# Rotating 96 images by 90 degrees: six hand-synchronised groups of 16 with 32 KB runs, in place of pooled tiles with 8 KB and 16 KB runs

## The chip, the cores and the metric

The kernel runs on one core of a Trainium2 chip. The metric is the device time of one execution in microseconds; a lower number is better. Before the change the median of three executions is 124.25 us.

## The reference

```python
x: float32 [32, 3, 256, 256]
out = np.rot90(x, k=1, axes=(-2, -1))     # out[.., i, j] = x[.., j, 255 - i]
```

96 images of 256 x 256 float32 (256 KB each) are rotated a quarter turn. No arithmetic is done: 25.17 MB are read and 25.17 MB are written, and every image is transposed and reversed along one axis on the way.

## The kernel before, in words

**Groups.** The 96 images are six groups of 16 images (4 MB each), and a group goes through three steps: DMAs bring it from DRAM into a tile `S` [128 partitions x 8192 float32], VectorE transposes `S` into a tile `U` of the same size, DMAs write `U` to DRAM. VectorE's transpose exchanges 32 partitions with 32 elements of the free dimension, so the access patterns `src` and `dst` choose which 32 elements meet and apply the reversal. `S` and `U` come from pools of three buffers each, so three groups can be in flight on either side. SyncE (SP) issues the loads, ScalarE (ACT) the stores; each has a DMA queue of its own, and both queues feed the same 16 DMA engines. In the profile the loads are queue q1 and the stores queue q10.

**Two kinds of group.** `KINDS = [1, 2, 2, 2, 2, 1]`.
- Kind 1 (the first and the last group): a partition holds 8 image rows, one run of 8 KB in DRAM. The group is cut into four quarters `s` of 1 MB: four loads (L50), four transposes of 128 x 2048 (L55), each followed by its store (L56). A quarter is transposed and stored as soon as it has landed.
- Kind 2 (the four groups between): a partition holds 16 image rows, one run of 16 KB. Two loads of 2 MB (L66), sixteen transposes of 128 x 512 (L71), each reading from both halves, then two stores of 2 MB (L73). The first transpose needs both loads.

**Zeros.** Ahead of the groups VectorE clears a tile `zero` [128 x 128] (L35) and ACT writes it, 64 KB in pieces of 512 B, to the part of the output that the last store overwrites at the end (L37).

**Order.** Tiles and semaphores are the tile framework's. It makes a load wait until the buffer that it overwrites was read, a transpose until its loads have landed and the old `U` was stored, and a store until its transposes are done. L88 and L99 are the framework's start and end.

Of the kernel before, what the change touches and what calls it, by code (L numbers as in the profile page):

```python
# [1 line left out]

# [4 lines left out]


@with_exitstack
def kernel(  # L10
    ctx: ExitStack,
    tc: tile.TileContext,
    x: bass.AP,
    out: bass.AP,
):
    nc = tc.nc
    B, C, H, W = x.shape
    assert H == W == 256
    N = B * C
    P = 128  # L20
    G = 16
    KINDS = [1, 2, 2, 2, 2, 1]
    assert len(KINDS) * G == N
    F = G * H * W // P
    fp32 = mybir.dt.float32

    xf = x.rearrange("b c h w -> (b c h w)").rearrange("(g f) -> g f", g=N // G)
    of = out.rearrange("b c h w -> (b c h w)").rearrange("(g f) -> g f", g=N // G)

    in_pool = ctx.enter_context(tc.tile_pool(name="in_pool", bufs=3))  # L30
    out_pool = ctx.enter_context(tc.tile_pool(name="out_pool", bufs=3))


    zero = ctx.enter_context(tc.tile_pool(name="zero", bufs=1)).tile([P, 128], fp32, name="zero")
    nc.vector.memset(zero[:], 0.0)  # L35
    last = of[N // G - 1].rearrange("(s p f) -> s p f", s=4, p=P)[3]
    nc.scalar.dma_start(out=last[:, :128], in_=zero[:])  # L37

    for g, kind in enumerate(KINDS):
        S = in_pool.tile([P, F], fp32, name="S")  # L40
        U = out_pool.tile([P, F], fp32, name="U")
        if kind == 1:

            R = 8
            Sv = S.rearrange("p (s f) -> p s f", s=4)
            Uv = U.rearrange("p (s f) -> p s f", s=4)
            xv = xf[g].rearrange("(s p f) -> s p f", s=4, p=P)
            ov = of[g].rearrange("(s p f) -> s p f", s=4, p=P)
            for s in range(4):
                nc.sync.dma_start(out=Sv[:, s], in_=xv[s])  # L50
            for s in range(4):

                src = Sv[:, s].rearrange("p (r k q) -> p q r k", r=R, q=R)[:, ::-1, :, ::-1]
                dst = Uv[:, s].rearrange("p (q k r) -> p q r k", q=R, r=R)
                nc.vector.transpose(dst, src)  # L55
                nc.scalar.dma_start(out=ov[s], in_=Uv[:, s])  # L56
        else:


            R = 16  # L60
            Sv = S.rearrange("p (b f) -> p b f", b=2)
            Uv = U.rearrange("p (a f) -> p a f", a=2)
            xv = xf[g].rearrange("(b a qk f) -> b qk a f", b=2, a=2, f=F // 2)
            ov = of[g].rearrange("(b a qk f) -> a qk b f", b=2, a=2, f=F // 2)
            for b in range(2):
                nc.sync.dma_start(out=Sv[:, b], in_=xv[b])  # L66

            src = Sv.rearrange("p b (r k q) -> p q r k b", r=R, q=R)[:, ::-1, :, ::-1]
            dst = Uv.rearrange("p a (q k r) -> p q r k a", q=R, r=R)
            for q in range(R):  # L70
                nc.vector.transpose(dst[:, q], src[:, q])  # L71
            for a in range(2):
                nc.scalar.dma_start(out=ov[a], in_=Uv[:, a])  # L73


# [1 line left out]
_INS = ['x']  # L77
_OUTS = [((32, 3, 256, 256), 'float32')]


# [23 lines left out]
```

## Time and profile before

| | |
|---|---|
| times of three runs | 124.26, 124.12, 124.25 us (median 124.25) |
| the profiled execution | 124.26 us, of which the span from first to last instruction is 122.5 us |
| VectorE busy | 91.5 us (75% of the span), 73 instructions |
| loads, queue q1 | 2304 packets, 25.17 MB |
| stores, queue q10 | 2448 packets, 25.23 MB (the zeros are in it) |
| moved over the span | 50.41 MB, mean 412 GB/s |

How to read it: the span is what the trace covers, and 1.76 us of the execution's time lie around it. The share of a DMA queue is the time that its packets took, added up over the 16 engines, as a share of 16 times the span. A packet here is one contiguous run of data, or a 4-byte semaphore write: each DMA adds 16 of those, one for each engine. The line of tenths cuts the span into 40 slices of 3.06 us. "To landing" is the time from the issue of a DMA to the semaphore that reports it complete. "Issue" is time in which an engine waited for nothing that the profile shows.

### The profile page before, as it was taken

What the parts mean: (1) busy time and instruction counts of PE and PEld (TensorE: products, weight loads), DVE (VectorE), ACT (ScalarE), POOL (GpSimd) and SP (SyncE); (2) the same over time, 40 slices, a digit from 0 to 9 for tenths busy, and PEclk for the clock granted to TensorE, in tenths of its full rate; (3) what the DMA queues carried; (4) which work ended last, traced back from release to release, by engine and by line L of the source; (5) the groups of instructions that cost most, each with busy time, mean ns of one, the idle gap of its engine ahead of it and who ended that gap; (6) DMA issues with size and microseconds to landing.
All of it is one profiled execution on the core that took longest, in us unless ns stands there. A gap on an engine that the chain in (4) does not pass through costs nothing.

```text
span 122.5 us, 173 instructions
## 1 busy us (share of the span) xinstructions
DVE 91.5 (75%) x73; POOL 0.2 (0%) x4
## 2 busy tenths in 40 slices
DVE  0199999006999999999999991699999999191000
POOL 0000000000000000000000000000000000000000
DMA  3999999999999999999999999999999999999994
GB/s 99 420 428 407 409 399 431 449 420 417 452 399 433 460 433 342 428 428 428 428 428 450 439 439 423 425 447 399 433 439 415 452 433 407 455 433 393 428 428 185
DMA packets 4753, 50.41 MB, mean 412 GB/s; under 512 B 528, under 2 KB 656, under 8 KB 656
## 3 DMA queue, kind: packets, MB, share of 16 engines
q1 hardware_dynamic: 2304, 25.17, 49.3%
q10 hardware_dynamic: 2448, 25.23, 48.4%
q14 instruction: 1, 0.01, 0.0%
HBM read 25.17 MB, written 25.23 MB: 411 GB/s over the span
## 4 chain that ended last, share of the span: by engine, by line
DMA 69%; DVE 20%; SPq 0%; issue 0%
DMA S<-in_x_dram 38%; DMA out_dram<-U 31%; DVE U L55 13%; DVE U L71 8%; SPq L50 0%
## 5 line engine op out<-in xcount | busy, mean ns | idle before, releaser
L71 DVE STREAM_TRANSPOSE U<-S 128x512 f32<-128x512 f32 x64 | 60.5, 1049 | 11.1 <-DMA S<-in_x_dram 7.4
L55 DVE STREAM_TRANSPOSE U<-S 128x2048 f32<-128x2048 f32 x8 | 31.0, 3948 | 7.2 <-DMA S<-in_x_dram 7.2
L35 DVE MEMSET zero<- 128x128 f32 x1 | 0.2, 165 | 0.8 <-PEq L88 0.8
L88 POOL MEMSET const-bfloat16-1.0<- 128x1 bf16 x1 | 0.1, 103 | 0.0
L88 POOL MEMSET const-uint8-127<- 128x1 uint8 x1 | 0.1, 103 | 0.0
L88 POOL MEMSET const-float32-1.0<- 128x1 f32 x1 | 0.1, 100 | 0.0
L88 POOL MEMSET const-float32-0.0<- 128x1 f32 x1 | 0.1, 99 | 0.2 <-issue 0.2
## 6 DMA issues: line engine op xcount, KB each, us to landing
S<-in_x_dram SPq DMA_DIRECT2D x8, 2048.0 KB, 21.5
out_dram<-U ACTq DMA_DIRECT2D x8, 2048.0 KB, 19.1
S<-in_x_dram SPq DMA_DIRECT2D x8, 1024.0 KB, 16.4
out_dram<-U ACTq DMA_DIRECT2D x8, 1024.0 KB, 15.9
out_dram<-zero ACTq DMA_DIRECT2D x1, 64.0 KB, 5.0
```

Of the source, the lines that this page charges most:

```text
L35: nc.vector.memset(zero[:], 0.0)
L55: nc.vector.transpose(dst, src)
L71: nc.vector.transpose(dst[:, q], src[:, q])
L88: nc = _bacc.Bacc("TRN2", target_bir_lowering=False, num_devices=1)
```

## The change

The pools and the framework's tracking go. Three buffers `S0..S2`, three buffers `U0..U2` and seven semaphores are named by hand: `loaded[s]` and `stored[u]` count DMA completions (16 each), `turned` counts groups that VectorE has finished. A block for hand-written code (`tile_critical`) stands around it all.

All six groups have one form now. Of each MB block `b` a partition of `S` holds 8 image rows, and the four blocks lie side by side in it: four loads of 1 MB. In the first group they are plain loads of 128 runs of 8 KB. In the other five the DRAM side of the load is written as 32 runs of 32 KB and the SBUF side as 128 partitions of 8 KB; since the usual call takes equal shapes on both sides, the instruction is built directly (`load`). VectorE turns a group in eight transposes of 128 x 1024, one for each image row `r` in a partition, each reading from all four blocks. A partition of `U` then holds 32 image rows, and one store of 4 MB writes 128 runs of 32 KB.

The waits: a load of group `g` from 3 on waits until group `g - 3` is turned; the first transpose of a group waits for its four loads and, from group 3 on, for the store of group `g - 3`; the store waits for the last of the eight transposes. At the end SP waits for all stores. The zeros (tile, clearing and write) are gone.

```diff
@@ -18,59 +18,77 @@
     assert H == W == 256
     N = B * C
     P = 128
-    G = 16
-    KINDS = [1, 2, 2, 2, 2, 1]
-    assert len(KINDS) * G == N
-    F = G * H * W // P
+    M = 4
+    G = 4 * M
+    RI, RO = 8, 8 * M
+    KO = H // RO
+    FI, FO = RI * W, RO * W
+    FOLD = 32
+    NG = N // G
+    NS = NU = 12 // M
     fp32 = mybir.dt.float32
 
-    xf = x.rearrange("b c h w -> (b c h w)").rearrange("(g f) -> g f", g=N // G)
-    of = out.rearrange("b c h w -> (b c h w)").rearrange("(g f) -> g f", g=N // G)
+    xf = x.rearrange("b c h w -> (b c h w)")
+    of = out.rearrange("b c h w -> (b c h w)")
 
-    in_pool = ctx.enter_context(tc.tile_pool(name="in_pool", bufs=3))
-    out_pool = ctx.enter_context(tc.tile_pool(name="out_pool", bufs=3))
+    xv = xf.rearrange("(g b d f) -> g b d f", g=NG, b=M, d=FOLD)
+    xp = xf.rearrange("(g b p f) -> g b p f", g=NG, b=M, p=P)
+
+    ov = of.rearrange("(g b qk f) -> g qk b f", g=NG, b=M, f=FO)
+
+    def fixed(ap):
+        return mybir.PhysicalAccessPattern(
+            ap=ap.ap, offset=ap.offset, dtype=ap.dtype, memref=ap.tensor.name,
+            memsetref=ap.tensor.name + "_set", bass_ap=ap,
+        )
+
+    def load(dst, src):
 
 
-    zero = ctx.enter_context(tc.tile_pool(name="zero", bufs=1)).tile([P, 128], fp32, name="zero")
-    nc.vector.memset(zero[:], 0.0)
-    last = of[N // G - 1].rearrange("(s p f) -> s p f", s=4, p=P)[3]
-    nc.scalar.dma_start(out=last[:, :128], in_=zero[:])
+        return nc.sync.add_instruction(
+            mybir.InstDMACopy(
+                name=nc.get_next_instruction_name(),
+                engine=mybir.EngineType.SP,
+                ins=[fixed(src)],
+                outs=[fixed(dst)],
+                queue="qSPDynamicHW",
+                mode="Copy",
+            )
+        )
 
-    for g, kind in enumerate(KINDS):
-        S = in_pool.tile([P, F], fp32, name="S")
-        U = out_pool.tile([P, F], fp32, name="U")
-        if kind == 1:
+    ctx.enter_context(tc.tile_critical())
+    S = [ctx.enter_context(nc.sbuf_tensor(f"S{i}", [P, M, FI], fp32)) for i in range(NS)]
+    U = [ctx.enter_context(nc.sbuf_tensor(f"U{i}", [P, FO], fp32)) for i in range(NU)]
+    loaded = [ctx.enter_context(nc.semaphore(f"loaded{i}")) for i in range(NS)]
+    stored = [ctx.enter_context(nc.semaphore(f"stored{i}")) for i in range(NU)]
+    turned = ctx.enter_context(nc.semaphore("turned"))
 
-            R = 8
-            Sv = S.rearrange("p (s f) -> p s f", s=4)
-            Uv = U.rearrange("p (s f) -> p s f", s=4)
-            xv = xf[g].rearrange("(s p f) -> s p f", s=4, p=P)
-            ov = of[g].rearrange("(s p f) -> s p f", s=4, p=P)
-            for s in range(4):
-                nc.sync.dma_start(out=Sv[:, s], in_=xv[s])
-            for s in range(4):
+    for g in range(NG):
+        s, u = g % NS, g % NU
+        if g >= NS:
+            nc.sync.wait_ge(turned, g - NS + 1)
+        for b in range(M):
+            if g == 0:
+                d = nc.sync.dma_start(out=S[s][:, b], in_=xp[g, b])
+            else:
+                d = load(S[s][:, b], xv[g, b])
+            d.then_inc(loaded[s], 16)
 
-                src = Sv[:, s].rearrange("p (r k q) -> p q r k", r=R, q=R)[:, ::-1, :, ::-1]
-                dst = Uv[:, s].rearrange("p (q k r) -> p q r k", q=R, r=R)
-                nc.vector.transpose(dst, src)
-                nc.scalar.dma_start(out=ov[s], in_=Uv[:, s])
-        else:
+        nc.vector.wait_ge(loaded[s], 16 * M * (g // NS + 1))
+        if g >= NU:
+            nc.vector.wait_ge(stored[u], 16 * (g // NU))
 
+        src = S[s][:].rearrange("p b (r k q) -> p r q k b", r=RI, q=RO)[:, :, ::-1, ::-1]
+        dst = U[u][:].rearrange("p (q k r) -> p r q k", q=RO, r=RI)
+        for r in range(RI):
+            t = nc.vector.transpose(dst[:, r], src[:, r])
+        t.then_inc(turned, 1)
 
-            R = 16
-            Sv = S.rearrange("p (b f) -> p b f", b=2)
-            Uv = U.rearrange("p (a f) -> p a f", a=2)
-            xv = xf[g].rearrange("(b a qk f) -> b qk a f", b=2, a=2, f=F // 2)
-            ov = of[g].rearrange("(b a qk f) -> a qk b f", b=2, a=2, f=F // 2)
-            for b in range(2):
-                nc.sync.dma_start(out=Sv[:, b], in_=xv[b])
+        nc.scalar.wait_ge(turned, g + 1)
+        nc.scalar.dma_start(out=ov[g], in_=U[u][:]).then_inc(stored[u], 16)
 
-            src = Sv.rearrange("p b (r k q) -> p q r k b", r=R, q=R)[:, ::-1, :, ::-1]
-            dst = Uv.rearrange("p a (q k r) -> p q r k a", q=R, r=R)
-            for q in range(R):
-                nc.vector.transpose(dst[:, q], src[:, q])
-            for a in range(2):
-                nc.scalar.dma_start(out=ov[a], in_=Uv[:, a])
+    for u in range(NU):
+        nc.sync.wait_ge(stored[u], 16 * len(range(u, NG, NU)))
 
 
 # ---- launch: one core; inputs and outputs as the reference has them ----
```

## The prediction

> **What bounds the kernel now.** The page comes first: is any resource full from end to end?
>
> ```profile
> span 122.5 us, 173 instructions
> DVE 91.5 (75%) x73; POOL 0.2 (0%) x4
> DVE  0199999006999999999999991699999999191000
> DMA  3999999999999999999999999999999999999994
> q1 hardware_dynamic: 2304, 25.17, 49.3%
> q10 hardware_dynamic: 2448, 25.23, 48.4%
> ```
>
> VectorE has holes; the DMA row has none between the first slice and the last. The queue shares add to 97.7% of 16 engines: 0.977 x 122.5 = 119.7 us of packets on each engine. The rest is start and end. The windows view of half microseconds places it:
>
> ```profile
> 1.00:1.50 0.50, 0.00 (x0) 0.00 (x0) 1.00 0.00 0
> 1.50:2.00 0.50, 0.00 (x0) 0.00 (x0) 1.00 0.49 131
> ...
> 120.50:121.00 0.50, 0.00 (x0) 0.00 (x0) 1.00 0.50 213
> 121.00:121.50 0.50, 0.00 (x0) 0.00 (x0) 1.00 0.09 33
> ```
>
> The last two columns are the DMA share and GB/s. Packets run from about 1.7 to about 121.3; 1.7 us lie before, 1.2 after. So the DMA engines set the time, and VectorE's 91.5 us hide beneath them. The chain of waits says so too: it is 69% DMA, and its VectorE pieces lie where the engines work on for other buffers.
>
> Next, what a packet costs and how the two queues share an engine. I asked for the DMA queues between 90 and 104 us, where loads are 8 KB packets (kind 1) and stores 16 KB (kind 2):
>
> ```profile
> q10 hardware_dynamic: 273, 3.95, 65.9%
> q1 hardware_dynamic: 275, 1.99, 33.6%
> ```
>
> Columns: packets, MB, share. Equal packets (32 of each are semaphore writes), twice the bytes: **the engines alternate packet by packet**, and a queue with smaller packets gets less. Shares times 16 x 14 us, over 243 and 241 data packets: 0.310 us for 8 KB, 0.612 us for 16 KB. The difference is 0.302 us per 8 KB, which leaves some 0.007 us fixed for each packet; 32 KB would take 4 x 0.302 + 0.007 = 1.216 us.
>
> Then VectorE, from the groups:
>
> ```profile
> L71 DVE STREAM_TRANSPOSE U<-S 128x512 f32<-128x512 f32 x64 | 60.5, 1049 | 11.1 <-DMA S<-in_x_dram 7.4
> L55 DVE STREAM_TRANSPOSE U<-S 128x2048 f32<-128x2048 f32 x8 | 31.0, 3948 | 7.2 <-DMA S<-in_x_dram 7.2
> ```
>
> 60.5/4 = 15.1 us for a kind 2 group and 31.0/2 = 15.5 us for a kind 1 group. Different strides, nearly the same price for an element, 1.85 to 1.89 ns.
>
> [...] the L71 transposes lie between 1021 and 1083 ns under full DMA traffic.
>
> **The change, part by part.**
>
> *DMA work.* Per engine, before: 64 + 64 packets of 8 KB at 0.309 and 64 + 64 of 16 KB at 0.611 make 117.8; 33 semaphore writes, 0.3; the zeros, 8 of 512 B, at most 0.2. Sum 118.3; the 119.7 of the page holds 1.4 us more, load packets that run slower than their floor. After: 32 of 8 KB (first group) are 9.9, 40 + 48 of 32 KB are 107.0, 30 semaphore writes 0.3: 117.2. So **1.1 us of packet time go**. The lower bound is 0.3 (if a widened load pays for four 8 KB writes, 40 x 0.024 = 1.0 comes back, and only the stores and zeros gain).
>
> *Memset, zeros' issue, pool waits.* The clearing is 0.165 us at L35, under the first load; its end is awaited only by the zeros' write. I take nothing beyond the packet time above.
>
> *The order of work.* Group 0 no longer starts transposing after 1 MB but after 4. By hand, with 15.3 us a group on VectorE:
> - Load 0 from 1.7 to 11.6, landed at 11.9. VectorE turns groups 0, 1, 2 back to back until 27.2, 42.5, 57.8.
> - Meanwhile loads 1 and 2 keep the engines full (8 x 1.216 = 9.7 us a group): load 1 lands at 21.6. Store 0 starts moving at 28.5 (1.3 us after its issue; the first load of before needed 0.73 to about 1.7), and halves load 2's rate: 33.8. So VectorE's later first start costs nothing, because three buffers of loads (29 us) cover it.
> - Now both queues always have work with 32 KB packets and alternate: 19.5 us for 4 MB on each. Loads 3, 4, 5 land at 53.2, 72.7, 92.1; stores 0, 1, 2 at 47.1, 66.6, 86.0. The load's new wait on `turned` holds SP only, with nothing else queued there, and comes due at 27.2, 42.5, 57.8, ahead of need.
> - VectorE: group 3 from 57.8 to 73.1, group 4 to 88.4, group 5 waits for its load and runs 92.2 to 107.5.
> - From 92.1 the engines have only stores. Left are 6.7 us of store 3 and 9.7 of store 4: to about 108.8. Store 5 is issued at 107.5 and moves at 108.8. **It comes just in time.** It ends at 118.6, the span at 119.8.
>
> The same arithmetic for before gives 1.7 + 118.3 + 1.2 = 121.2 against a true 122.5. I carry most of that remainder, 1.2, since loads run alone for longer here.
>
> *Entry and end of the hand-written block.* The program gains a branch and a no-op with a semaphore on SP, ACT and VectorE at both ends. Nothing in the trace prices it; what is there is the start, where the first DMA follows its branch within 0.1 us, and the end, 0.7 us of framework after the last landing. Between 0 and 1 us; I take 0.3. Less than nothing is excluded, as nothing of the framework's start and end is removed.
>
> Sum: 119.8 + 1.2 + 0.3 = 121.3 us of span, with 1.76 around it 123.1; a tenth for a gap ahead of store 5 gives **123.2 us**. The profiled execution (124.26) stands at the median (124.25), so no correction. A measurement here can tell about 0.2%, 0.25 us: under 124.0 is faster, over 124.5 slower.
>
> **The rivals.**
>
> *Loads still count as 8 KB packets* (slower). If the engine splits the widened read by its 8 KB writes, it sends 8 KB of load for 32 KB of store. For it: the SBUF side is 8 KB, and the 33.6% against 65.9% show what unequal packets do. [...] The stores run dry early and the loads are late: load 5 lands near 102.7 in place of 92.1. Group 5 has no pieces, so all that follows is bare: 15.3 of VectorE, 1.3 to first data, 9.7 of store, 1.2 of end: 130.3, with a remainder of 0.5 and 1.76, about **132.5 us**. It decides as soon as load 5 is later than about 92, since then the engines idle ahead of store 5.
>
> *VectorE's turn takes longer* (slower). The slack ahead of store 5 is about nil, but faster or slower turns also shift when loads are handed over; worked again with longer turns, no gap opens up to 15.9 us a group; from there each further microsecond of a group costs about 6, since all six follow one another. At 16.5 (2.0 ns an element) that is 123.2 + 3.4 = **126.6**. For it: the stride of 8 KB between the four blocks is new. Against it: kinds 1 and 2 differ in stride and hardly in price. An uneven sharing between the queues, or slower widened loads, would land in the same place, 125 to 129.
>
> *The change gives nothing* (same). Four writes are paid for each widened packet (+1.0) and entry and end cost 0.3 more than taken: **124.5 us**, between 123.8 and 124.8.
>
> **How the numbers follow.** Forecast 0.64, holding 122.2 to 124.6 (faster 0.54, same 0.06, slower 0.04). 8 KB packets 0.15, at 131 to 134, slower. VectorE or sharing 0.14, slower. Nothing gained 0.07 (0.02, 0.03, 0.02). So faster 0.56, same 0.09, slower 0.35. The range runs from 122.2 (no entry cost, half of the remainder) to 129, and leaves out the 8 KB case and the edges. The likeliest case alone: 122.2 to 124.6.
>
> **What would show it.** Right: q1's rate between 35 and 85 us equals q10's; DMA tenths of 9 throughout, also ahead of the last store; transposes near 1.9 us each, six groups of 15.3; group 5 starting near 92. Queue shares that add to less than before. Wrong: q1 at a fifth of the bytes in the shared stretch and a hole of ten microseconds near 110 (8 KB packets); eight transposes over 15.9 us and no wait for loads (VectorE); packets full but their total near 119.7 (nothing gained); a first DMA well after 1.0 us (entry).

## The result, and the profile after

The changed kernel takes 132.07 us (median of four runs, 131.71 to 136.57) against 124.19 before. The ratio is 1.0625, with a 95% interval of 1.0591 to 1.0658: slower by 7.8 us by the ratio, with the median 3.1 us above the upper end of the range forecast (129). A few runs here lie some 4 to 5 us above the others of the same kernel; ratios leave them out, medians don't, and the traces of `e4_tail_pieces` and `e10_store_2mb` are of such runs.

The page of the changed kernel, the lines that answer to those of before:

```profile
span 130.2 us, 134 instructions
DVE 91.0 (70%) x48; POOL 0.2 (0%) x4
...
DVE  0000999999999999999999607999900699990000
...
DMA  3999999999899999999999999999999997007973
...
q1 hardware_dynamic: 1536, 25.17, 46.1%
q10 hardware_dynamic: 864, 25.17, 44.9%
```

The DMA row has a hole that before had not, in the slices from about 107 to 120 us. The shares add to 91.0% of 130.2 us, 118.5 us on each engine, where before had 119.7 by the same sum. So the packets did become cheaper, by about what was forecast, and the engines stood idle for longer than that saved. The windows view places the idle stretch (columns: VectorE busy, POOL busy, clock, DMA share, GB/s):

```profile
108.00:110.00 2.00, 2.00 (x3) 0.00 (x0) 1.00 0.99 426
110.00:112.00 2.00, 2.00 (x2) 0.00 (x0) 1.00 0.08 33
112.00:114.00 2.00, 2.00 (x2) 0.00 (x0) 1.00 0.00 0
114.00:116.00 2.00, 2.00 (x2) 0.00 (x0) 1.00 0.00 0
116.00:118.00 2.00, 1.43 (x1) 0.00 (x0) 1.00 0.00 0
118.00:120.00 2.00, 0.00 (x0) 0.00 (x0) 1.00 1.16 492
```

While the engines stand still, VectorE turns the last group. The timeline says when it could begin (columns: start, length, engine, line, the idle time ahead and what ended it):

```profile
13.22 60.47 DVE L84 STREAM_TRANSPOSE U<-S 128x1024 f32<-128x1024 f32 x32 [13.22 <-DMA S<-in_x_dram]
...
78.82 15.24 DVE L84 STREAM_TRANSPOSE U<-S 128x1024 f32<-128x1024 f32 x8 [5.13 <-DMA S<-in_x_dram]
102.17 15.25 DVE L84 STREAM_TRANSPOSE U<-S 128x1024 f32<-128x1024 f32 x8 [8.11 <-DMA S<-in_x_dram]
```

Group 5 begins at 102.2 where the forecast had 92.2, and it waits for its load. From there everything is bare: 15.2 us of VectorE, 1.3 to the first packet, some 10 of store, 1.6 of end. **The loads came ten microseconds late.** Why is in the queues between 35 and 85 us, where both have work (packets, MB, share):

```profile
q10 hardware_dynamic: 422, 12.26, 56.8%
q1 hardware_dynamic: 432, 9.44, 43.9%
```

The number of packets is nearly the same again, but not the bytes. With 32 KB each, 9.44 MB are 288 data packets and 12.26 MB are 374. What fills up the 432 and the 422 are semaphore packets: 144 for the loads and 48 for the stores. The trace's packet records don't name the engine, but they show the order on one when each packet is put behind the one that ends where it starts, to within 4 ns (L, S: 32 KB of load or store; l, s: their 4-byte semaphore writes; one engine from 38 us on; the chains of the others run alike):

```
LSLSlSLSLSlsLSLSlSLSLSlSLSLSlsLSLSlSLSLSlSLSLSlsLS
```

A turn is the one packet that an engine takes from a queue before it goes to the other. After each two load packets (with a store packet between them and one behind) comes `l`, and after `l` a store packet: the 9 ns semaphore write takes the loads' turn and the store then has 1.2 us. A load of 1 MB is two data packets and one semaphore packet on an engine; a store of 4 MB is eight and one. So of three turns the loads use two for data, of nine the stores eight: 0.667 against 0.889, 42.9% of the bytes. Measured are 9.44/21.70 = 43.5%.

### The profile page after: what moved, and what is told of

Same layout as the page of the kernel before. It is cut to its first block, busy times and chain, and to the rows that moved or that the text cites. A ratio compares the mean times of both kernels' runs of the same rounds, so it can differ in the third digit from the quotient of the medians.

```text
span 130.2 us, 134 instructions
## 1 busy us (share of the span) xinstructions
DVE 91.0 (70%) x48; POOL 0.2 (0%) x4
## 4 chain that ended last, share of the span: by engine, by line
DVE 45%; DMA 40%; SPq 3%; issue 2%
DVE U L84 45%; DMA S<-in_x_dram 40%; SPq L48 2%; SPq L72 1%; SPq L117 0%; SPq L59 0%
## 5 line engine op out<-in xcount | busy, mean ns | idle before, releaser
L84 DVE STREAM_TRANSPOSE U<-S 128x1024 f32<-128x1024 f32 x48 | 91.0, 2060 | 26.5 <-DMA S<-in_x_dram 26.5
```

Source lines behind the costliest of these rows:

```text
L84: t = nc.vector.transpose(dst[:, r], src[:, r])
```

## The experiments

The theory to test: **the alternation gives a semaphore packet a whole turn, so the queue with more semaphores per byte loses.** It is called the turn theory below. Rivals: the widened load (32 runs of 32 KB read into 128 partitions) holds its own queue back, the widening theory; the loss is the last group's single piece, whatever the sharing, the tail theory.

### Stores of 1 MB (`e1_store_1mb`)

```diff
-        nc.scalar.dma_start(out=ov[g], in_=U[u][:]).then_inc(stored[u], 16)
+        for b in range(M):
+            nc.scalar.dma_start(out=ov[g][:, b], in_=U[u][b::M]).then_inc(stored[u], 16)
```

The waits on `stored` count four times as far.

> Each 4 MB store is cut into four of 1 MB (every fourth partition), so a store has 2 data packets and 1 semaphore packet per engine, as a load has. Turn theory (an engine's alternation gives a semaphore packet a whole turn, so the queue with more semaphores per byte loses): both queues move equal bytes in the shared stretch, load 5 lands near 94, the engines idle about 1 us, span 121.4, time 123.3. Widening theory (a read of 32 KB with four writes holds its queue back by itself): the loads keep about 43% of the bytes, time stays near 132. Tail theory (handing over the last group in one piece costs by itself, whatever the sharing): a hole near 110 stays, time near 132.

Measured: 124.35 us, ratio 1.0015 (0.9998 to 1.0031). Eighteen more DMAs, and 7.6 us less by the ratios. The queues from 35 to 80 us:

```profile
q1 hardware_dynamic: 446, 9.90, 51.3%
q10 hardware_dynamic: 433, 9.47, 48.9%
```

the DMA row of its page:

```profile
DMA  2999989899998989898999898999999999999991
```

and the last group in the timeline:

```profile
92.29 15.26 DVE L84 STREAM_TRANSPOSE U<-S 128x1024 f32<-128x1024 f32 x8 [3.44 <-DMA out_dram<-U]
```

The bytes are even, group 5 begins at 92.3, and it no longer waits for its load but for an old `U` to be stored. The DMA row has no hole. The loads are the same widened ones as in the changed kernel: the widening theory falls. VectorE turns the last group in the same one piece, and its stores wait for the end of it: the tail theory falls as a cause by itself. The span missed its mark, 122.3 for 121.4, and the time likewise; that is taken up below.

### One load of 4 MB for a group (`e11_one_load`)

```diff
-        for b in range(M):
...
-                d = load(S[s][:, b], xv[g, b])
-            d.then_inc(loaded[s], 16)
+            xg = xf.rearrange("(g p b f) -> g p b f", g=NG, b=M, p=P)[g]
+            nc.sync.dma_start(out=S[s][:], in_=xg).then_inc(loaded[s], 16)
```

Group 0 keeps its four loads.

> The other side of the 1 MB stores: the stores stay whole (8 data packets and 1 semaphore packet per engine) and the loads of groups 1 to 5 become one DMA of 4 MB each, 128 runs of 32 KB to 128 partitions, also 8 and 1. The rows then lie otherwise in the partitions, so the output isn't the rotation: that part of the computation is changed, the amount of data and the instructions of VectorE are not. Turn theory: equal bytes on both queues in the shared stretch, no hole, packet time about 118 per engine, time 124.2 like the 1 MB stores. A theory in which short stores let the loads in, and not the count of semaphores per byte, expects the sharing to stay at 43% and the time at 132.

Measured: 124.36 us, ratio 1.0014 (1.0005 to 1.0022). From 35 to 80 us:

```profile
q1 hardware_dynamic: 334, 9.90, 51.0%
q10 hardware_dynamic: 322, 9.50, 49.0%
```

Here nothing of the stores is changed, and the time comes out the same as with 1 MB stores. It is not the cutting of stores that helps, but the same count of semaphores per byte on both sides. (These loads are also not widened, which alone would leave the widening theory open; the experiment before has ruled it out.)

### Stores of 2 MB (`e10_store_2mb`)

```diff
+        for b in range(2):
+            nc.scalar.dma_start(out=ov[g][:, b::2], in_=U[u][b::2]).then_inc(stored[u], 16)
```

> A size between the changed kernel and the 1 MB stores: each 4 MB store is cut into two of 2 MB (every second partition), so a store has 4 data packets and 1 semaphore packet per engine. Turn theory, by count: a load gets 2/3 x 32 KB a turn, a store 4/5 x 32 KB, so loads have 45.5% of the bytes in the shared stretch (43% and 50% in the two kernels beside it); load 5 lands near 96.5, the engines idle some 2 to 3 us ahead of the last store, span near 124.7, time 126.8. A theory in which any cut of the store lets the loads in evenly expects 50% and 124.3; one in which only equal DMAs help expects no change from 132.

Measured: 127.29 us, ratio 1.0250 (1.0237 to 1.0264). From 35 to 80 us:

```profile
q10 hardware_dynamic: 398, 10.42, 54.1%
q1 hardware_dynamic: 398, 8.85, 46.5%
```

Exactly as many packets on both sides; 8.85/19.27 = 45.9% of the bytes for 45.5 by count, and the time lies between those of the two neighbours, near the 126.8 expected. So cutting as such doesn't make the sharing even, and stores that are still longer than the loads gain too. Where load 5 lands in a run of that length is not on record.

### Stores of 16 KB runs (`e3_store_16k`)

```diff
+        for h in range(2):
+            c = slice(h * FO // 2, (h + 1) * FO // 2)
+            nc.scalar.dma_start(out=ov[g][:, :, c], in_=U[u][:, c]).then_inc(stored[u], 16)
```

> Each store is cut into two of 2 MB with runs of 16 KB (half of a partition each); loads stay. Turn theory: load 2/3 x 32 KB a turn, store 8/9 x 16 KB, so loads get 60% of the bytes, load 5 lands near 83, group 5 no longer waits for its load, no hole ahead of the last store, span 120.6, time 122.7. Widening theory: loads remain behind, time 127 to 132. Tail theory: near 132.

Measured: 127.78 us, ratio 1.0294 (1.0277 to 1.0310). The sharing is as the theory has it, 11.54/19.40 = 59.5%, with 528 packets on each queue:

```profile
q1 hardware_dynamic: 528, 11.54, 59.9%
q10 hardware_dynamic: 528, 7.86, 40.9%
```

But the time expected is missed by 5 us. What VectorE waited for:

```profile
DVE U L84 <- DMA S<-in_x_dram: 13.3, 1, 13.3
DVE U L84 <- DMA out_dram<-U: 3.4, 1, 3.4
...
```

are the waits of the 1 MB stores, and these are the waits here (time, times, longest):

```profile
DVE U L84 <- DMA S<-in_x_dram: 13.2, 1, 13.2
DVE U L84 <- DMA out_dram<-U: 8.8, 1, 8.8
```

Group 4 waits until 82.4 for a `U` buffer, because the stores are now the starved side. My sum started the first store 1.3 us after its issue, and in the trace its first packet comes at 33.6, 5.1 us after. By an estimate from these figures, without the 3.8 us between the two the wait would end near 78.6 and the last group would be turned near 109, before the engines run out of older stores near 111. As it is, the last group ends late and the engines idle for 2.8 us. The rest of the 5 us is packet time (119.2 us on an engine) and the start and end that are priced below. Of the shares tried, the even ones are the fastest.

### Plain loads of 8 KB packets (`e2_plain_loads`)

```diff
-            if g == 0:
+            if True:
```

> All loads are plain, 8 packets of 8 KB per engine and MB, stores stay 32 KB. Turn theory: per cycle of turns a load has 8/9 x 8 KB against 8/9 x 32 KB of the store, a fifth of the bytes while both queues have work; but the stores then run dry and the loads have the engines alone between them, so load 5 lands near 101, the engines idle some 7 us, span 128.2, time 130.3: no worse than the widened loads. Widening theory: without widening the loads lose nothing, time near 123. If the widening is worth what its smaller share suggests (20% against 43%), the time is well over 132.

Measured: 133.59 us, ratio 1.0748 (1.0714 to 1.0781). This is what the rival of the forecast described. It is slower than the widened loads, against what I expected of it, but by only 1.5 us: the stores run dry in between (998 packets of loads to 403 of stores from 35 to 80 us), so the loads catch up, and group 5 begins at 104.9 where the widened loads allow 102.2. Load 5 was expected near 101; why it is later is not shown. Of the 9.1 us between this kernel and the 1 MB stores with widened loads, widening alone gives 1.5; the rest comes only when the semaphore counts are made equal.

### The last group in four pieces (`e4_tail_pieces`), and with 1 MB stores (`e5_1mb_tail`)

```diff
+        n = NT if g == NG - 1 else 1
+        for h in range(n):
+            e = slice(h * RO // n, (h + 1) * RO // n)
+            for r in range(RI):
+                t = nc.vector.transpose(dst[:, r, e], src[:, r, e])
+            t.then_inc(turned, 1)
...
+                nc.scalar.dma_start(out=ov[g][:, :, c], in_=U[u][:, c]).then_inc(stored[u], 16)
```

> Only the last group is changed: it is turned in four quarters of columns (8 transposes of 128 x 256 each) and each quarter is stored as soon as it is turned, in runs of 8 KB. Turn theory: sharing as in the changed kernel, load 5 still near 102; the first quarter moves at 108, before the engines run out of stores near 110; the last is turned at 118.2 and ends near 122; span 123.1, time 125.2: most of the loss returns though nothing of the sharing is mended. Tail theory: back to 123 or below. A theory in which the loss lies anywhere but ahead of the last store expects no gain, 131 to 132.

Measured: ratio 1.0088 (1.0068 to 1.0108), from two runs of 125.23 and 125.28 us, as expected.

> Both remedies together: stores of 1 MB and the last group in quarters. Turn theory: with even sharing the last group is turned while older stores still move, so its one piece is hidden and the quarters have nothing to win; 124.4, within 0.3 of the 1 MB stores alone. Tail theory as an effect of its own (about 6 us for the pieces wherever they are): well under 123.

Measured: 124.46 us, ratio 1.0032 (1.0020 to 1.0044). So the pieces are worth 6.7 us by the ratios where the loads are late and nothing where they are not. The two causes don't add: late loads make the hole, and the single piece sets how long it is.

### Zeros (`e7_before_no_zeros`) and the hand-written block (`e8_before_block`)

```diff
-    zero = ctx.enter_context(tc.tile_pool(name="zero", bufs=1)).tile([P, 128], fp32, name="zero")
-    nc.vector.memset(zero[:], 0.0)
...
-    nc.scalar.dma_start(out=last[:, :128], in_=zero[:])
```

> The kernel before without the zeros (tile, clearing, 64 KB write), that part of the change alone. Packet theory: 0.2 us of packet time go, 124.0, hardly to be told from no change. Warming theory (the early small write makes the store queue's first real store start sooner): without it the stores start later and the time rises by up to 1 us; but a queue behind a backlog starts late anyway and the engines stay full, so even then no change in time.

Measured: 124.08 us, ratio 0.9992 (0.9984 to 1.0000). Dropping the zeros is worth at most 0.2 us; the first store issued at 9.48 had its first packet at 13.1, no later after its issue than with the zeros (9.75 and 13.9). No warming is seen.

```diff
+    with tc.tile_critical():
+        nc.vector.nop()
+        nc.scalar.nop()
+        nc.sync.nop()
```

> The kernel before with a hand-written block around one no-op on each of VectorE, ACT and SP, placed after the last store, so that the block's entry and end are both paid in the open. If the block costs what the traces suggest (first packet 0.3 later, 0.45 more after the last packet, 0.35 more around the span), the time rises by 1.1 to 125.3. If it costs the 0.3 that the prediction took, 124.5. If nothing, 124.2.

Measured: 126.92 us, ratio 1.0229 (1.0216 to 1.0242), but it doesn't answer the question. The framework placed the block ahead of the last three transposes, where it waits for all loads: VectorE's line shows it, 11.7 us of idle time that the block's line on SP ended.

```profile
L55 DVE STREAM_TRANSPOSE U<-S 128x2048 f32<-128x2048 f32 x8 | 31.0, 3939 | 16.5 <-SPq L75 11.7
```

So the price of the block is not isolated; what the traces say of it stands below.

### The packet saving without the block (`e12_kinds_2`, `e13_kinds_2_1`)

```diff
-    KINDS = [1, 2, 2, 2, 2, 1]
+    KINDS = [2, 2, 2, 2, 2, 2]
```

and for the second `[2, 2, 2, 2, 2, 1]`, both without the zeros.

> The kernel before without the zeros and with all six groups of kind 2: no 8 KB packets, 96 loads and 96 stores of 16 KB per engine, 117.3 and 24 semaphore packets 0.2: 117.5 against 118.0 with two groups of kind 1. Loads and stores both have 8 data packets per semaphore, so they share evenly to the end, load 5 lands near 92 and the last group's turn is hidden under older stores, as with the 1 MB stores; no block for hand-written code. Time 123.6. If the last group's single piece is not hidden (load 5 later than 93), the engines idle ahead of the last store: 124 to 128.

> The same with the last group left as kind 1: its 8 KB loads get a third of the bytes against 16 KB stores, its quarters are turned and stored as they land. Packet time 117.8 per engine; the engines stay full to the end as in the kernel before. Time 123.8, between 123.6 and 124.1.

Measured: 124.60 us, ratio 1.0028 (1.0020 to 1.0036), and 125.08 us, ratio 1.0066 (1.0054 to 1.0078). They miss by 1.0 and 1.3 us. The sharing is right (9.68 and 9.70 MB for the first), and its last group begins at 93.4 with no hole at the end. Set against the trace of before, the first kernel's packets take 0.51 us less on an engine (119.60 to 119.09) where some 0.7 was summed; but its first packet comes 0.36 us later (2.11 for 1.75) and the engines idle 0.69 us more, which makes the profiled execution 0.54 us longer. The second's packets take only 0.10 us less, its first packet comes 0.39 later, the engines idle 0.37 more, and 0.18 more passes after the last packet. Both begin with a load of 2 MB where before begins with one of 1 MB; whether that makes the first packet late is not shown, nor where the idle time comes from.

## Why the prediction was wrong, point by point

- **What bounds the kernel, price of a packet: right.** The widened load packet has a median of 1.221 us and the 32 KB store packet of 1.213, for 1.216 worked out. In the records it is one packet of 32 KB (640 of them for the twenty widened loads); that it would be one was the author's assumption, since before has no such load. It doesn't pay four times the fixed part, which would make it 4 x 0.309 = 1.236: plain 32 KB loads (`e11_one_load`) have a median of 1.213. Packets went from 119.6 to 118.5 us on an engine, 1.1 as summed. The alternation read from before holds as well: an engine switches after each single run, of 32 KB on both queues in `LSLS` above, of 8 KB against 16 KB in the 273 and 275 packets of before.
- **VectorE: right.** 15.2 to 15.3 us a group for 15.3; its rival falls. The last three transposes of the changed kernel ran while the engines stood still and took 2.01 to 2.05 us each; those of the group before, under full traffic, took 2.02 to 2.10. All 48 lie between 2.01 and 2.12 us with a median of 2.06, so DMA traffic costs a transpose at most some 0.1 us here.
- **The step that failed: "Now both queues always have work with 32 KB packets and alternate: 19.5 us for 4 MB on each."** It counted a semaphore packet at its 9 ns and not at its turn. The last packets of loads 3, 4 and 5 came at 54.1, 77.1 and 100.5, 23 us apart, where 19.5 was taken. The line between 90 and 104 us that carried the step, 273 packets against 275, contains 32 semaphore packets on each side: there the counts were equal and the effect could not show. In the changed kernel they are 1 in 3 against 1 in 9. So group 5 began at 102.2 in place of 92.2, and what followed was bare, as the prediction's own condition "later than about 92" says.
- **"It comes just in time": right as a warning.** With even sharing (`e1_store_1mb`, `e11_one_load`) group 5 begins at 92.3 and 92.2, and the engines are not idle ahead of the last store: with 1 MB stores the group is turned at 107.6 and older stores run to 110.9.
- **The rival of the 8 KB packets had the time (132.5) and not the cause.** Packets were 32 KB, and the loads had 43%, not a fifth, of the bytes. Its time was met by luck: it had load 5 at 102.7 for another reason. Run as a kernel of its own, it takes 133.59. The 43% belong to the clause "An uneven sharing between the queues", which I put at 125 to 129. There the sum for a load 5 ten microseconds late, which that rival has, was not applied.
- **Start and end: too small, and their cause is open.** With even sharing the forecast would still have been 1.1 us too low: 124.35 for 123.2. From before to `e1_store_1mb`, in their traces: first packet 1.75 to 2.02 us (+0.28), packets on an engine 119.60 to 118.34 (-1.26), engines idle between first and last packet +0.29, last packet to end of span 1.14 to 1.65 (+0.51), time around the span 1.79 to 2.14 (+0.35). Rounding apart, this is the 0.16 by which the profiled executions differ (124.42 - 124.26). So 1.1 us went at the start, at the end and around the span, where 0.3 was taken for entry and end of the block. The block doesn't explain all of it: `e4_tail_pieces` and `e5_1mb_tail` stand in the same block, and in all their runs 1.7 to 1.8 us lie around the span, as before; and `e12_kinds_2`, without the block, has its first packet at 2.11. The longer end fits the block best: 1.55 to 1.65 us in every kernel that lies in it, 1.14 to 1.32 in those that don't. No run isolates it.
- **First store moving at 28.5: wrong, without harm here.** It moved at 33.9 in the changed kernel. Until then the loads had the engines to themselves (88 packets to none from 28.5 to 33 us); a loss is seen only where stores were the starved side (`e3_store_16k`).
- **Slips in the sums, without weight.** From its own steps (4 MB need 9.7 us, half rate from 28.5 on) store 0 lands at 48.0 and not 47.1, and engines that are full from 1.7 on end at 118.9 and not 118.6. And if 1.0 us of the 1.1 comes back, 0.1 is left and not 0.3.

No kernel of this study beats the kernel before by more than it can be told; the one without zeros comes closest.

## What to carry to other kernels

When two DMA queues share busy engines, count turns and not bytes: data packets plus one semaphore packet per DMA, on each engine. In the kernels here a queue's bytes went as its packet size times the share of data packets in its turns. While both queues had work, this gave the loads' share to about a point, counted against measured: 42.9 and 43.5% in the changed kernel, 45.5 and 45.9 with 2 MB stores, 50 and 51.1 with 1 MB stores, 50 and 51.0 with one load of 4 MB, 60 and 59.5 with 16 KB runs. With packets of one size, cut both sides alike: the loads fell behind, at 43.5 and 45.9%, where they were the shorter DMAs. Then ask of the side that falls behind what hangs on its last piece: here a load of the last group that came ten microseconds late exposed VectorE's turn of 15.2 us and a whole store of some 10, and the same pieces were free once the loads came in time (124.35 us).

## What the hardware showed that was not expected

- A semaphore write of 9 ns takes a full turn in the alternation and so gives the other queue 1.2 us (`LSLSlS` above). Each DMA here ends in one such packet on each engine (480 for the 30 DMAs of the changed kernel, on 16 engines), so the runs don't tell the packet from the end of a DMA as the cause of the lost turn.
- A store on a queue that was empty, beside a backlog on the other queue, had its first packet late: issued at 28.52 and moving at 33.9 in the changed kernel, 28.47 and 32.5 with `e5_1mb_tail`, 9.75 and 13.9 before. On idle engines it took 1.2 (117.46 and 118.7). From 28.5 to 33 us in the changed kernel the records have 88 packets of loads and none of stores. What holds the store back is not shown.
